# A third seven-product block in the wide products of three feed-forward steps, shared sums written back into their banks, and W_uq's rope columns multiplied once

## The chip, the cores and the metric

One Trainium2 chip, one core of it. The metric is the time of one execution of the whole program on the device in microseconds (us), the lower the better. The core works with several engines side by side: TensorE (PE in the profile; its weight loads are PEld), VectorE (DVE), ScalarE (ACT), GpSimd (POOL), and SyncE (SP), which issues nearly all transfers (DMAs) here. Each engine runs its own instructions in a fixed order and waits for others by semaphores.

## What is computed

A decoder trunk of two layers for 256 tokens, width 1024, in fp32:

```python
h = h + 0.5 * swiglu(rms_norm(h, ffn1_norm), ffn1_w_gate, ffn1_w_up, ffn1_w_down)   # D_FF = 2816
u = rms_norm(h, mix_norm)
...  # proj = u @ w_in; stick-breaking attention (8 heads of 64)
q = (rms_norm(c_q, q_lat_norm) @ w_uq).reshape(b, s, MLA_HEADS, MLA_QK_DIM)     # 4 heads of 128 + 64
q_nope, q_rope = q[..., :MLA_NOPE_DIM], q[..., MLA_NOPE_DIM:]
q_rope = apply_rope(q_rope, cos[:, None, :], sin[:, None, :])
...  # latent attention, output projection
h = h + 0.5 * swiglu(rms_norm(h, ffn2_norm), ffn2_w_gate, ffn2_w_up, ffn2_w_down)
gate = jax.nn.sigmoid(rms_norm(h, ple_norm) @ w_ple_gate)
h = h + gate * (p_i @ w_ple_proj)
```

`swiglu(x)` is `(silu(x @ w_gate) * (x @ w_up)) @ w_down`, and `apply_rope` turns the two halves of 32 of each 64: `x1*cos - x2*sin` and `x2*cos + x1*sin`.

## The kernel before

The work is a sequence of four feed-forward steps (tags a0, b0, a1, b1, here steps 1 to 4), each layer's mixing stage behind its first step and its per-layer embedding behind its second. The 256 tokens are two halves of 128, and a block of outputs is 512 columns wide, the last of the six blocks 256.

**Products.** fp32 is made of three products of a faster format: each operand is split in a high part and the rest, and `mm3` (L255 to L266) issues three matmuls, wh·xh (L262), wl·xh (L263) and wh·xl (L264). A weight tile of 128x1024 takes one DMA of 512 KB into a raw buffer (7 of them), an ACT copy that rounds it to wh (L158, or L199 in a seven-product), and a DVE subtraction wl = raw − wh (L159 or L200). wh and wl have 8 buffers each. PE needs both.

**A plain block** of gate and up: 8 weight tiles, 96 matmuls of 512 columns into four banks of PSUM (g and u for each half of the tokens). Then ACT makes silu(g) (L565), DVE the product pr (L569) and its transpose (L541); a DMA into memory and four back (L543, L548) turn it, and ACT and DVE split the turned tile into fh and fl (L524, L525). DVE also adds up sums of turned tiles for the down projection (L485 to L497).

**A wide seven-product block** (`wide_seven`, L599) replaces a part of these products by the seven products of a 2 x 2 block scheme (Strassen-Winograd): the halves of the tokens and of the inner dimension on one side; a gate and an up tile on the other. Four weight tiles of class `Seven` become seven operands by four sums of raw tiles on DVE (L194), in the order 1, 7, 6, 5, 2, 4, 3 (`operands_own_first`, L220). Products 1, 7, 6 and 5 start the banks p1, p7, p6 and p5; 2 adds onto p1, 4 onto p7, 3 onto p5. Sums that several outputs share are made beside the banks: u is a copy of p1 (ACT, L613), then DVE adds p6 to u (L615), makes v = u + p7 (L616) and e = p5 − v (L618). The other half of the inner dimension comes as ordinary products (`half_mm`, L621): the gate unit ug onto p1 and p7, the up unit uu onto p5 and onto a fresh bank c22. DVE finishes the outputs with v = u + p7 (L628), u = p5 − u (L631) and e = e + c22 (L632). The block has 90 matmuls, and 11 instead of 8 subtractions for wl. `wide_sevens` (L53) names the blocks that are done in this way: 3 in the first step, 1 and 3 in the others. The down projection uses sevens of its own (`SEVEN`), which the change leaves alone.

**W_uq in the mixing stage** (L903 to L921). `qs` are four banks. Its eight groups of 128 columns, each with two `mm3` of 256 columns, are four groups for the nope part, two for the rope part (qs[2]) and two for the same rope columns in rotated order (qs[3]). DVE makes r1 = qs[2]·cos (L917) and r2 = qs[3]·sin (L919), the sign of the rotation in the sine's table, and POOL adds both to qr (L921), which the scores (L945 and after) use beside kn (L930) and qn (L912). Later the attention's output is normed (L882), turned by PE (L893) and projected.

**What sets the order.** The program is written as one sequence; a scheduler places the instructions of each engine by priorities, with hand-set due times (`soon`, `tick`, counted in PE time, L255 ff.) for the pieces that follow a block, such as the turning of pr. `r(1.4)` moves that piece later by 1.4 us.

## Time and profile before

| | |
|---|---|
| three runs | 989.3, 989.6 and 990.46 us, median 989.6 |
| the profiled execution | 989.71 us, of which the span is 987.9 us |
| mean granted clock of PE | 0.997 |
| PE, DVE, ACT busy | 977.5, 850.4, 652.3 us |
| matmuls | 4904 |
| 512 KB weight tiles loaded | 338, 5.2 us from issue to landing |

The span is the time from the first to the last instruction of the profiled execution; 1.8 us lie around it. Rows of the timeline are start, duration, engine, line, operation, output <- inputs and shape; a bracket at the end is idle time ahead of the row and what ended it. An "x2" means two instructions in one row. Names in the trace leave out numbers: all tiles of steps 2 and 4 have a b, those of steps 1 and 3 an a. Durations of neighbours on one engine can overlap, since a pipeline starts the next before the last has ended, so what an instruction costs is read from the starts.

### The profile page before, as it was taken

The page shows a single profiled execution, that of the slowest core. Times are in us where ns is not written, and L with a number is a line of the kernel's source. Part 1 is how long each engine was busy: PE and PEld are TensorE (multiplying, and loading weights), DVE is VectorE, ACT ScalarE, POOL GpSimd, SP SyncE. Part 2 cuts the span into 40 slices and gives each one's busy share as a digit, 9 for nine tenths or more (in the row PEclk, how much of TensorE's full clock was granted, in tenths as well). Part 3 has the DMA queues.
Part 4 walks back from the last instruction along what each step waited for, and adds up shares of the span by engine and source line. Part 5 has one row for each costly group of instructions (what it writes and reads, how often), then busy time and mean ns, then how long its engine had stood idle before and what let it go on. Part 6 is the DMA issues. An engine that isn't in the chain of part 4 may idle for free.

```text
span 987.9 us, 14025 instructions
## 1 busy us (share of the span) xinstructions
PE 977.5 (99%) x4904; PEld 826.0 (84%) x4904; DVE 850.4 (86%) x1130; ACT 652.3 (66%) x1003; POOL 9.3 (1%) x13
## 2 busy tenths in 40 slices
PE   9999999999999999999999999999999999999996
PEld 7888888899888888888888888889998888888885
DVE  5799899966779998999889989998676899989994
ACT  5856566857577566657876655667766766656673
POOL 0000000000100000000000000000010000000000
PEclk9999999999999999999999999999999999999998
DMA  8948766765244788666647776668623367876641
GB/s 292 337 183 290 247 200 218 252 236 169 77 138 140 252 261 302 172 227 233 214 139 281 232 270 210 211 226 291 208 87 128 107 214 249 282 235 205 219 163 43
DMA packets 85175, 208.40 MB, mean 211 GB/s; under 512 B 13680, under 2 KB 33264, under 8 KB 85104
## 3 DMA queue, kind: packets, MB, share of 16 engines
q1 hardware_dynamic: 84672, 206.93, 62.5%
q8 instruction: 38, 0.62, 0.3%
q10 hardware_dynamic: 432, 0.57, 0.2%
q14 instruction: 33, 0.27, 0.1%
HBM read 195.94 MB, written 11.53 MB: 210 GB/s over the span
## 4 chain that ended last, share of the span: by engine, by line
PE 91%; ACT 3%; DVE 3%; DMA 2%; issue 1%; SPq 0%; ACTq 0%; DVEq 0%
PE p_b L262 3%; PE p_b L264 3%; PE p_b L263 3%; PE p_a L262 3%; PE p_a L264 3%; PE p_a L263 3%; PE d_a L264 3%; PE d_b L262 3%; PE d_b L263 3%; PE d_a L263 3%; PE d_a L262 3%; PE d_b L264 3%; PE g_b L262 3%; PE g_b L263 3%; PE g_b L264 3%; PE g_a L264 2%
## 5 line engine op out<-in xcount | busy, mean ns | idle before, releaser
L159 DVE TENSOR_TENSOR wl<-raw,wh 128x1024 fp32r<-128x1024 f32 (+1 forms) x278 | 324.3, 1191 | 61.8 <-ACT wh L158 58.5
L158 ACT ACTIVATE wh<-raw 128x1024 fp32r<-128x1024 f32 (+1 forms) x278 | 281.9, 1038 | 109.0 <-DMA raw<-in_w 21.1
L199 ACT ACTIVATE wh<-raw 128x1024 fp32r<-128x1024 f32 x133 | 139.2, 1059 | 112.7 <-DVE raw L194 70.4
L200 DVE TENSOR_TENSOR wl<-raw,wh 128x1024 fp32r<-128x1024 f32 x133 | 160.8, 1219 | 9.9 <-ACT wh L199 8.1
L194 DVE TENSOR_TENSOR raw<-raw,raw 128x1024 f32<-128x1024 f32 x76 | 92.3, 1219 | 2.0 <-DMA raw<-in_w 1.5
L262 PE MATMUL d_b<-wh,fh_b 128*128 128x512 f32 x108 | 42.4, 392 | 0.0
L262 PE MATMUL d_a<-wh,fh_a 128*128 128x512 f32 x108 | 42.4, 392 | 0.0
L264 PE MATMUL d_b<-wh,fl_b 128*128 128x512 f32 x108 | 42.1, 389 | 0.0
L264 PE MATMUL d_a<-wh,fl_a 128*128 128x512 f32 x108 | 42.1, 389 | 0.0
L263 PE MATMUL d_a<-wl,fh_a 128*128 128x512 f32 x108 | 42.0, 389 | 0.0
L263 PE MATMUL d_b<-wl,fh_b 128*128 128x512 f32 x108 | 42.0, 389 | 0.0
L262 PE MATMUL g_a<-wh,x0h 128*128 128x512 f32 x80 | 31.3, 393 | 0.0
L263 PE MATMUL g_a<-wl,x0h 128*128 128x512 f32 x80 | 31.1, 391 | 0.2 <-DVE wl L159 0.2
L264 PE MATMUL g_a<-wh,x0l 128*128 128x512 f32 x80 | 31.0, 390 | 0.0
L263 PE MATMUL u_a<-wl,x0h 128*128 128x512 f32 x64 | 25.2, 393 | 0.2
L262 PE MATMUL g_b<-wh,x_mix0h 128*128 128x512 f32 x64 | 25.0, 391 | 0.0
L262 PE MATMUL g_b<-wh,x_mix1h 128*128 128x512 f32 x64 | 25.0, 391 | 0.0
L263 PE MATMUL g_b<-wl,x_mix1h 128*128 128x512 f32 x64 | 25.0, 391 | 0.0
L262 PE MATMUL g_a<-wh,xe0h 128*128 128x512 f32 x64 | 25.0, 391 | 0.0
L263 PE MATMUL g_b<-wl,x_mix0h 128*128 128x512 f32 x64 | 25.0, 391 | 0.0
L262 PE MATMUL u_a<-wh,x0h 128*128 128x512 f32 x64 | 24.9, 392 | 0.0
L264 PE MATMUL u_a<-wh,x0l 128*128 128x512 f32 x64 | 24.9, 390 | 0.0
(561 smaller groups left out, 2681.7 us busy)
## 6 DMA issues: line engine op xcount, KB each, us to landing
raw<-in_w SPq DMA_DIRECT2D x338, 512.0 KB, 5.2
m_b<-pr_b SPq DMA_DIRECT2D x20, 256.0 KB, 2.5
ft_b<-m_b SPq DMA_DIRECT2D x80, 64.0 KB, 3.0
raw<-in_w SPq DMA_DIRECT2D x16, 256.0 KB, 4.5
m_a<-pr_a SPq DMA_DIRECT2D x16, 256.0 KB, 2.4
ft_a<-m_a SPq DMA_DIRECT2D x64, 64.0 KB, 2.7
xin<-in_xT SPq DMA_DIRECT2D x4, 256.0 KB, 5.1
h<-in_xr SPq DMA_DIRECT2D x2, 512.0 KB, 8.9
```

Of the source, the lines that this page charges most:

```text
L158: nc.scalar.activation(wh[:, a], r[:, a], AF.Copy),
L159: nc.vector.tensor_tensor(wl[:, a], r[:, a], wh[:, a].bitcast(F32), ALU.subtract),
L194: nc.vector.tensor_tensor(self.raw[o], self.raw[a], self.raw[b], op)
L199: newest_wh[0] = nc.scalar.activation(wh, r, AF.Copy)
L200: nc.vector.tensor_tensor(wl, r, wh.bitcast(F32), ALU.subtract)
L262: nc.tensor.matmul(o, ah, bh, start=start, stop=False, **kw)
L263: nc.tensor.matmul(o, ah, bl, start=False, stop=False, **kw)
L264: newest_mm[0] = nc.tensor.matmul(o, al, bh, start=False, stop=stop, **kw)
```

## The change

Three things change.

1. `wide_sevens` adds block 4 in steps 2 to 4, so the three steps have sevens at 1, 3 and 4. Step 1 keeps block 3.
2. In every wide seven the sums are written back into banks: u = u + p6 and v = u + p7 as before; then ACT copies v into bank p7, DVE writes p5 − v into bank p6 and p5 − u into bank p5. From there on all products (2, 4, 3 and both halves of `half_mm`) add onto the four banks, and silu and pr read the banks themselves. The bank c22, the tile e and the three late DVE sums are gone; the delay of 1.4 us is gone too.
3. W_uq is multiplied without the rotated columns (six groups, not eight; the weight unit is filled up with zeros). r2 is made of four DVE operations of 32 partitions, each of which reads the neighbouring group of 32 rows of qs[2]; the sine's table has its signs swapped.

```diff
-    return (3,) if first else (1, 3)
+    return (3,) if first else (1, 3, 4)
...
-            e2 = tuple(f_p.tile([P, 4, T], F32, tag=f"f5{q}", name=f"c{q}_{tag}{i}").rearrange("p a b -> p (a b)") for q in "hl")
-            u, v, e = e2[0][:, :512], e2[0][:, 512:], e2[1][:, :512]
+            e2 = f_p.tile([P, 4, T], F32, tag="f5h", name=f"c_{tag}{i}").rearrange("p a b -> p (a b)")
+            u, v = e2[:, :512], e2[:, 512:]
...
                 elif q == 6:
                     nc.vector.tensor_tensor(u, u, p[6], ALU.add)
                     nc.vector.tensor_tensor(v, u, p[7], ALU.add)
+                    nc.scalar.copy(p[7], v)
                 elif q == 5:
-                    nc.vector.tensor_tensor(e, p[5], v, ALU.subtract)
-            c22 = bank(f"c22_{tag}{i}")
+                    nc.vector.tensor_tensor(p[6], p[5], v, ALU.subtract)
+                    nc.vector.tensor_tensor(p[5], p[5], u, ALU.subtract)
...
-                        mm3(banks[t], tok(x, 4 + k, t), u.at(k, 0, 512), banks[t] is c22 and k == 0, k == 3, skip_group_check=True)
+                        mm3(banks[t], tok(x, 4 + k, t), u.at(k, 0, 512), False, k == 3, skip_group_check=True)
...
             half_mm(ug, (p[1], p[7]))
-            nc.vector.tensor_tensor(v, u, p[7], ALU.add)
-            rests = [gated(i, 0, p[1], u)[1], gated(i, 1, v, e)[1]]
-            half_mm(uu, (p[5], c22))
-            nc.vector.tensor_tensor(u, p[5], u, ALU.subtract)
-            nc.vector.tensor_tensor(e, e, c22, ALU.add)
+            rests = [gated(i, 0, p[1], p[5])[1], gated(i, 1, p[7], p[6])[1]]
+            half_mm(uu, (p[5], p[6]))
             for r in rests:
-                r(1.4)
+                r()
...
-        qs = [pair(f"uq{L}_{i}") for i in range(4)]
-        for m in range(8):
+        qs = [pair(f"uq{L}_{i}") for i in range(3)]
+        for m in range(6):
...
-        nc.vector.tensor_tensor(r2, qs[3], bc(rc[:, 1], 2), ALU.mult)
+        for a in range(4):
+            to, of = (slice(32 * b, 32 * b + 32) for b in (a, a ^ 1))
+            nc.vector.tensor_tensor(r2[to], qs[2][of], rc[of, 1].unsqueeze(1).to_broadcast([32, 2, T]), ALU.mult)
...
-        units.append(cols(uq, np.r_[nope, rope, rotd]))
+        u = np.zeros((P, 2, UNIT // 2), uq.dtype)
+        u[:, :, :768] = cols(uq, np.r_[nope, rope]).reshape(P, 2, 768)
+        units.append(u.reshape(P, UNIT))
...
-    c[:, C_SIN : C_SIN + T] = np.concatenate([-sin, sin] * 2)
+    c[:, C_SIN : C_SIN + T] = np.concatenate([sin, -sin] * 2)
```

The scheduler answers to this with another order. First DVE in step 2, where block 2 ends and block 3 begins. A name holds the tile, the step (b0 is step 2), the block and the half; `wl7_59_3` is the operand in raw buffer 3 of the seven whose first weight unit is 59 (block 3), `wl61_0_0` the first tile of weight unit 61 (block 3's gate half), and pr_b0_20 the product of block 2, first half. Before:

```order
L200 TENSOR_TENSOR wl7_59_0_149_3598<-raw7_59_0_3523,wh7_59_0_149_3597 128x1024
L493 TENSOR_TENSOR sxl_b0_3398<-sum1_b0_1_3400,sxh_b0_3397 128x512
L200 TENSOR_TENSOR wl7_59_3_150_3622<-raw7_59_3_3538,wh7_59_3_150_3621 128x1024
L569 SCALAR_TENSOR_TENSOR pr_b0_20_3503<-u_b0_20_3329,hr_mix0_2812,s_b0_20_3427 128x512
L569 SCALAR_TENSOR_TENSOR pr_b0_21_3511<-u_b0_21_3330,hr_mix0_2812,s_b0_21_3429 128x512
L541 STREAM_TRANSPOSE pr_b0_20_3503<-pr_b0_20_3503 128x512
L541 STREAM_TRANSPOSE pr_b0_21_3511<-pr_b0_21_3511 128x512
L159 TENSOR_TENSOR wl61_0_0_151_3633<-raw61_0_0_151_3634,wh61_0_0_151_3632 128x1024
```

And DVE at the same place after the change:

```order
L493 TENSOR_TENSOR sxl_b0_3382<-sum1_b0_1_3384,sxh_b0_3381 128x512
L194 TENSOR_TENSOR raw7_59_0_3506<-raw7_59_0_3506,raw7_59_2_3569 128x1024
L569 SCALAR_TENSOR_TENSOR pr_b0_20_3487<-u_b0_20_3313,hr_mix0_2799,s_b0_20_3411 128x512
L569 SCALAR_TENSOR_TENSOR pr_b0_21_3495<-u_b0_21_3314,hr_mix0_2799,s_b0_21_3413 128x512
L541 STREAM_TRANSPOSE pr_b0_20_3487<-pr_b0_20_3487 128x512
L541 STREAM_TRANSPOSE pr_b0_21_3495<-pr_b0_21_3495 128x512
L200 TENSOR_TENSOR wl7_59_0_149_3583<-raw7_59_0_3506,wh7_59_0_149_3582 128x1024
L200 TENSOR_TENSOR wl7_59_3_150_3607<-raw7_59_3_3521,wh7_59_3_150_3606 128x1024
L616 TENSOR_TENSOR c_b03_3505<-c_b03_3505,p6_b03_3503 128x512
L159 TENSOR_TENSOR wl61_0_0_151_3617<-raw61_0_0_151_3618,wh61_0_0_151_3616 128x1024
```

The two last wl of block 3's seven-product stood ahead of the products of block 2 and now stand behind them. Next PE in block 4 of step 2. Before, a plain block begins there with

```order
L262 MATMUL g_b0_40_3725<-wh63_0_0_155_3729,x_mix0h_2809 128x512
L263 MATMUL g_b0_40_3725<-wl63_0_0_155_3730,x_mix0h_2809 128x512
L264 MATMUL g_b0_40_3725<-wh63_0_0_155_3729,x_mix0l_2810 128x512
L262 MATMUL g_b0_41_3726<-wh63_0_0_155_3729,x_mix0h_2809 128x512
L263 MATMUL g_b0_41_3726<-wl63_0_0_155_3730,x_mix0h_2809 128x512
```

After the change, the place where its seven-product gives way to the ordinary half (p1, p7, p6 and p5 are the banks, unit 63 belongs to the seven, 65 and 66 to the gate and up half):

```order
L264 MATMUL p7_b04_3707<-wh7_63_0_160_3787,x_mix0l_2797 128x512
L262 MATMUL p7_b04_3707<-wh65_0_0_162_3827,x_mix0h_2796 128x512
L262 MATMUL p6_b04_3708<-wh66_0_0_164_3867,x_mix0h_2796 128x512
L263 MATMUL p5_b04_3709<-wl7_63_3_161_3818,xsh_b0_3110 128x512
L264 MATMUL p5_b04_3709<-wh7_63_3_161_3817,xsl_b0_3111 128x512
L262 MATMUL p5_b04_3709<-wh7_63_3_161_3817,xsh_b0_3110 128x512
L263 MATMUL p5_b04_3709<-wl7_63_3_161_3818,xsh_b0_3110 128x512
L264 MATMUL p5_b04_3709<-wh7_63_3_161_3817,xsl_b0_3111 128x512
L262 MATMUL p5_b04_3709<-wh66_0_0_164_3867,x_mix0h_2796 128x512
L263 MATMUL p1_b04_3706<-wl65_0_0_162_3828,x_mix0h_2796 128x512
```

Matmuls with wh stand ahead of those with the wl of the same tile, several operands apart. The matmul with wl65_0_0_162 (the last row here) is the 137th from block 3's first. The third place is DVE in the first layer's mixing stage, before:

```order
L882 TENSOR_SCALAR on1_sb0_2464<-ov0_1_2312,tss_sb0_2450 128x512
L917 TENSOR_TENSOR r10_2536<-uq0_2_2468,rc0_2533 128x512
L919 TENSOR_TENSOR r20_2538<-uq0_3_2469,rc0_2533 128x512
L930 TENSOR_TENSOR kn0_2542<-kn0_0_2543,rl0_2423 128x512
L930 TENSOR_TENSOR kn0_2542<-kn0_1_2557,rl0_2423 128x512
```

and after:

```order
L881 TENSOR_SCALAR on1_sb0_2461<-ov0_1_2309,tss_sb0_2447 128x512
L916 TENSOR_TENSOR r10_2520<-uq0_2_2465,rc0_2517 128x512
L921 TENSOR_TENSOR r20_2522<-uq0_2_2465,rc0_2517 32x512 x4
L932 TENSOR_TENSOR kn0_2529<-kn0_0_2530,rl0_2420 128x512
L932 TENSOR_TENSOR kn0_2529<-kn0_1_2544,rl0_2420 128x512
```

One row on qs[3] has become four on groups of 32 rows of qs[2], ahead of both kn.

More of the change, by code (lines that the diff above doesn't have):

```diff
@@ L1184, in _weights @@
         rope = np.concatenate([192 * h + 128 + ar(64) for h in range(4)])
-        rotd = np.concatenate([192 * h + 128 + rot for h in range(4)])
-        units.append(cols(uq, np.r_[nope, rope, rotd]))
+        u = np.zeros((P, 2, UNIT // 2), uq.dtype)
+        u[:, :, :768] = cols(uq, np.r_[nope, rope]).reshape(P, 2, 768)
+        units.append(u.reshape(P, UNIT))
         ukv = i["w_ukv"][L]
```

## The prediction

> **What bounds the kernel now.** I read the page first: busy times, the clock row, the chain that ended last.
>
> ```profile
> PE 977.5 (99%) x4904; PEld 826.0 (84%) x4904; DVE 850.4 (86%) x1130; ACT 652.3 (66%) x1003; POOL 9.3 (1%) x13
> PEclk9999999999999999999999999999999999999998
> PE 91%; ACT 3%; DVE 3%; DMA 2%; issue 1%; SPq 0%; ACTq 0%; DVEq 0%
> ```
>
> TensorE (PE) is busy 99% of the 987.9 us span, at full clock, and carries 91% of the chain. Any matmul that goes should shorten the run by its pitch. But VectorE (DVE) is busy 86%, and 86% is a mean. So next I asked for busy time by windows of 10 us around block 3 of step 2 (columns: PE, weight loads, DVE, ACT, POOL busy, each with its count; clock; DMA share; GB/s).
>
> ```profile
> 340.00:350.00 10.00, 10.00 (x46) 8.29 (x45) 9.93 (x13) 6.51 (x9) 0.00 (x0) 1.00 0.73 235
> 350.00:360.00 10.00, 10.00 (x46) 8.29 (x45) 10.00 (x15) 7.31 (x9) 0.00 (x0) 1.00 0.78 256
> 360.00:370.00 10.00, 10.00 (x46) 8.29 (x45) 10.00 (x14) 6.02 (x8) 0.00 (x0) 1.00 0.79 239
> 370.00:380.00 10.00, 10.00 (x46) 8.29 (x45) 10.00 (x16) 6.90 (x9) 0.00 (x0) 1.00 0.84 322
> 380.00:390.00 10.00, 10.00 (x45) 8.27 (x45) 6.44 (x7) 5.65 (x7) 0.00 (x0) 1.00 0.88 258
> ```
>
> This is the reading that decides. Around one seven-product block DVE has no idle time for 40 us; it catches up only in the plain block behind it, after 380. Block 4, which is to become a seven-product block too, is that plain block.
>
> **Pitches.** The timeline of both engines there (start, duration, engine, line, instruction):
>
> ```profile
> 339.69 0.39 PE L263 MATMUL g_b<-wl,x_mix0h 128*128 128x512 f32 x1
> 354.20 0.39 PE L264 MATMUL u_b<-wh,x_mix0l 128*128 128x512 f32 x1
> 355.11 0.39 PE L262 MATMUL p_b<-wh,x_mix0h 128*128 128x512 f32 x1
> 375.51 0.39 PE L262 MATMUL g_b<-wh,x_mix0h 128*128 128x512 f32 x1
> 355.20 1.40 DVE L569 SCALAR_TENSOR_TENSOR pr_b<-u_b,hr_mix,s_b 128x512 f32<-128x512 f32 x2
> 356.52 1.29 DVE L541 STREAM_TRANSPOSE pr_b<-pr_b 128x512 f32<-128x512 f32 x2
> 357.74 2.31 DVE L159 TENSOR_TENSOR wl<-raw,wh 128x1024 fp32r<-128x1024 f32 x2
> 359.97 0.68 DVE L615 TENSOR_TENSOR ch_b<-ch_b,p_b 128x512 f32<-128x512 f32 x1
> 360.57 1.22 DVE L159 TENSOR_TENSOR wl<-raw,wh 128x1024 fp32r<-128x1024 f32 x1
> 361.71 0.68 DVE L616 TENSOR_TENSOR ch_b<-ch_b,p_b 128x512 f32<-128x512 f32 x1
> 344.90 1.22 DVE L194 TENSOR_TENSOR raw<-raw,raw 128x1024 f32<-128x1024 f32 x1
> 346.04 0.68 DVE L525 TENSOR_TENSOR fl_b<-ft_b,fh_b 128x512 fp32r<-128x512 f32 x1
> 346.64 1.22 DVE L194 TENSOR_TENSOR raw<-raw,raw 128x1024 f32<-128x1024 f32 x1
> 369.52 0.42 DVE L485 TENSOR_TENSOR sum_b<-ft_b 128x256 f32<-128x256 f32 x1
> 369.86 0.42 DVE L487 TENSOR_TENSOR sum_b<-ft_b,ft_b 128x256 f32<-128x256 f32 x1
> 378.86 2.32 DVE L159 TENSOR_TENSOR wl<-raw,wh 128x1024 fp32r<-128x1024 f32 x2
> ```
>
> Durations overlap, so I take start-to-start pitches. PE: 68 matmuls of 512 columns lie between 339.69 and 355.11, which is 0.2268 us each; the 90 of block 3 take 375.51 − 355.11 = 20.40, the same. DVE: a wl or a sum of two raw tiles 1.14 (360.57 to 361.71; 344.90 to 346.04), a 512-wide operation 0.60 (359.97 to 360.57), a 256-wide one 0.34 (369.52 to 369.86), pr 1.32 and the transpose 1.22 for the two (355.20 to 356.52, 356.52 to 357.74). A check: the order of before has, from the first pr to the wl at 378.86, 4 pr, 4 transposes, 10 wl, 9 512-wide and 5 256-wide operations: 2.64 + 2.44 + 11.40 + 5.40 + 1.70 = 23.58; the trace has 378.86 − 355.20 = 23.66. The sum of pitches is good to under 1%.
>
> **PE: three blocks.** A plain block has 96 matmuls, a seven-product one 90. Block 4 in three steps: 3 × 6 × 0.2268 = −4.08 us. Nothing else of the write-back touches PE's work, as the two halves that went to a bank of their own now add onto p5 and p6.
>
> **PE: W_uq.** 24 matmuls of 256 columns go, 12 a layer:
>
> ```profile
> 247.40 0.28 PE L263 MATMUL uq<-xqf5h,wh 128*128 128x256 f32 x1
> 253.03 0.28 PE L262 MATMUL kn<-xqf4l,wh 128*128 128x256 f32 x1
> 252.47 0.68 DVE L917 TENSOR_TENSOR r<-uq,rc 128x512 f32<-128x512 f32 x1
> 253.30 0.69 DVE L919 TENSOR_TENSOR r<-uq,rc 128x512 f32<-128x512 f32 x1
> 253.96 1.41 DVE L930 TENSOR_TENSOR kn<-kn,rl 128x512 f32<-128x512 f32 x2
> 256.74 0.39 PE L945 MATMUL s<-kn,qn 128*128 128x128 f32 x2
> 274.82 0.88 DVE L882 TENSOR_SCALAR on_mla<-os,tss_mla 128x512 f32<-128x512 f32 x2
> 275.79 0.60 PE L893 MATMUL yt_mla<-c_sb,on_mla 128*128 128x128 f32 x4
> ```
>
> 47 matmuls in 5.63 us, 0.1198 each, so PE reaches s 12 × 0.1198 = 1.44 earlier, at 255.3. But on DVE one r becomes four of 32 partitions; a row costs by its columns, so I take 0.60 each, and 0.69 as the upper bound. The first can follow the r at 252.47 at 253.07, the fourth ends its pitch at 255.47, and the two kn then end by 256.9 instead of 255.37. The first is done near 256.2, so PE waits some 0.9 and keeps 0.5. Even that has to pass a tie: on_mla ends at 275.70 and PE uses it at 275.79, at the end of a chain of softmax and norm, into which the new order puts two more wl. I take 0 per layer, with bounds of −1.44 (all of it counts) and +1.0 (the chain moves by the delay of kn). [...]
>
> **The write-back itself.** In blocks 1 and 3, v is now final after p6 and goes to bank p7 by an ACT copy. Product 4 adds onto p7 and so waits for this. Two rows show where before waited at that place:
>
> ```profile
> 320.04 0.50 PE L262 MATMUL p_b<-wh,x_mix0h 128*128 128x512 f32 x1
> 805.81 0.50 PE L262 MATMUL p_b<-wh,x_mix1h 128*128 128x512 f32 x1
> ```
>
> Those are late by 0.2 to 0.3 us, behind DVE in steps 2 and 4. In the new order product 4 stands six matmuls further back (1.36 us later), and by the pitches p7 is written at 8.65 us after the block's first matmul, against 38 × 0.2268 = 8.62 for its use: I take −0.25 for each of the two, bounds −0.3 and +0.5. DVE has two bank operations fewer per block. −0.5 together.
>
> **DVE in steps 2 and 4.** In the order after, from the first pr of block 2 up to wl65_0_0_162, the first weights of block 4 that belong to no seven-product, DVE has 4 pr, 4 transposes, 14 wl, 4 sums of raw tiles, 8 bank operations, 4 other 512-wide and 13 256-wide operations: 2.64 + 2.44 + 15.96 + 4.56 + 4.80 + 2.40 + 4.42 = 37.2 us. The first pr waits for the last matmul of u_b_20, three before the end of block 2 (354.20 + 0.39 = 354.59 in the timeline of before, 0.5 ahead of block 3's first matmul at 355.11). In front of that pr DVE has run dry: two wl of block 3 that stood ahead of it now stand behind, so DVE can't use the time up to u_b's end. wl65_0_0_162 is thus there 37.2 − 0.5 = 36.7 us after block 3's first matmul. PE, in its new order, asks for it 136 matmuls after that one: 136 × 0.2268 = 30.8. The difference, 5.9 us, is a stall of PE. The same sum gives 3.2 at wl7_63_0_160, so it comes in several pieces, none above 3 us. Behind wl65_0_0_162 each wl (1.14) feeds 12 matmuls (2.72), and DVE is ahead again. Two such steps: +12 us.
>
> What could hide it is a lead of DVE at that point. A lead would need free weight buffers: there are 8, and PE sets them free. ACT shows this in before, where its copy waits for PE's matmul:
>
> ```profile
> 336.32 1.06 ACT L199 ACTIVATE wh<-raw 128x1024 fp32r<-128x1024 f32 x1 [1.66 <-PE g_b L264]
> ```
>
> **DVE in step 3.** There the order keeps both wl of block 3 ahead of the first pr and puts the last sums of the down projection behind wl7_101_3_255. Up to that one DVE has 4 pr, 4 transposes, 11 wl, 4 sums, 8 bank operations, 3 512-wide and 5 256-wide ones, 30.5 us, so it is ready at 30.0; PE asks for it after 130 matmuls, at 29.5. I take +0.6, bounds 0 and +3.
>
> **Sum**, against the profiled execution's 989.7 us (the runs' median is 989.6, so the two agree): 989.7 − 4.1 − 0.5 + 0 + 12 + 0.6 = 997.7; I say 997.5 us. What a measurement can tell here from no change is about 0.2%, 2 us.
>
> **Rivals.**
> - *PE stays the only bound.* DVE keeps some 6 us more lead than the order lets me see, and all 42 matmuls count: 989.7 − 4.1 − 2.9 = 982.7, faster. For it: PE is 99% busy, and DVE has 3.6 us of 10 to spare after 380. Against: the pr that waits for u_b stands in front of the work that would build the lead. It decides if DVE gets through the 37.2 us in 31. Chance 0.17.
> - *Half the stall.* Part of the wl go faster or earlier, 3 us a step remain: 989.7 − 4.6 + 6 = 991.1, up to 994. Chance 0.13.
> - *A worse stall.* On SP's queue the raw tile of W 63_3 stands behind the transfers that turn block 2's products, and ACT copies into p7 in order, ahead of copies of weights that PE needs. What a late tile costs, the table of waits shows (total us, times, longest):
>
> ```profile
> ACT wh L158 <- DMA raw<-in_w: 21.1, 16, 4.3
> ```
>
>   The mean is 1.3 us. Two such waits in each of steps 2 to 4 give 997.7 + 3 × 2.6 = 1005.5 us; the longest in each gives 1010. Against: by the order the tile is asked for some 9 us (by the pitches) before DVE's turn to use it. The granted clock is 1.00 in every window above, so before shows no price of PE's gaps beyond their own length. [...] Chance 0.13.
> - *The change doesn't do what it says*: excluded by the order, which has 42 matmul rows fewer on PE.
>
> **How the numbers follow.** The forecast has 0.57, and by its own bounds (W_uq ± 2, write-back +1, step 3 +2.4, stall ± 2) 993 to 1003. The range reaches over half the stall (990) and to the worse stall (1006); what it leaves out is the first rival and the far end of the third. Faster by over 0.2%: the first rival and the edge of the second, 0.18. Within 0.2% (987.7 to 991.7): part of the second, 0.07. Slower: 0.75.
>
> **What would show it.** In the trace after, PE should have gaps of 1 to 3 us within block 4 of steps 2 and 4 (near 376 to 400 and 860 to 885), released by DVE wl (L200, then L159), about 6 us in each step; DVE should be busy 10.00 in every window of the 35 us before; step 3 should show at most 1 us; block 1's 0.3 us should be gone. In the mix, PE should wait for kn ahead of s by about 1 us. I am wrong if those gaps sum to less than 4 us in each step, or if DVE is not at 10.00 there; then PE's 7 us come through.

## The result, and the profile after

| | before | after |
|---|---|---|
| median of four runs | 989.65 us | 1012.86 us (1012.01 to 1013.83) |
| ratio to before, 95% interval | | 1.0234 (1.022 to 1.0247) |
| span of the profiled execution | 987.9 us | 1010.7 us |
| mean granted clock of PE | 0.997 | 0.993 |

The change costs 23.2 us. The forecast was 997.5 us, slower by 8, and its range ended at 1006: the sign was right and the size was off by a factor of three. The busy times, the clock row and the chain, from the page of after:

```profile
PE 983.6 (97%) x4862; PEld 822.0 (81%) x4862; DVE 875.8 (87%) x1155; ACT 663.3 (66%) x1025; POOL 8.5 (1%) x13
PEclk9999999999999999999999999999999999989999
PE 80%; DVE 11%; DMA 3%; issue 3%; ACT 3%; SPq 0%; DVEq 0%; ACTq 0%; POOL 0%; POOLq 0%
```

PE has the 42 matmuls fewer and is busy for longer, DVE's share of the chain has gone from 3% to 11%, and one slice of the clock row, in step 4, has dropped. The waits that PE itself shows are small. Total us, times and the longest, from the table of waits of after:

```profile
PE p_b L263 <- DVE wl L159: 4.3, 2, 2.2
PE s L947 <- DVE kn L932: 2.7, 2, 1.4
PE p_b L262 <- ACT wh L199: 2.6, 4, 0.8
PE yt_mla L892 <- DVE on_mla L881: 1.5, 2, 0.8
```

These come to 11.1 us. A wait before one matmul leaves out that the matmul behind it can take longer (0.50 us instead of 0.39 at 382.17 in step 2) and whatever a lower clock takes. So I compared the two executions by stages: from the first matmul of a stage to that of the next. Each entry is the stage's time less that in before, in us, from the profiled executions (the kernels beside after are told below; "b3-5" are blocks 3 to 5 of a step, "down" its down projection):

| stage (before, us) | after | no block 4 | old W_uq | W_uq alone | write-back alone | no block 4 in step 3 | block 4 without its sums | block 4 alone |
|---|---|---|---|---|---|---|---|---|
| mix 1 (109.30) | +1.74 | +1.74 | +0.03 | +1.75 | +0.03 | +1.77 | +1.76 | 0 |
| step 2, b0-2 (62.14) | −0.18 | −0.18 | −0.21 | −0.14 | −0.15 | −0.20 | −0.18 | −0.01 |
| step 2, b3-5 (53.04) | +5.33 | +0.29 | +5.90 | +0.20 | +1.81 | +5.54 | +0.85 | +1.90 |
| step 2, down (56.67) | +0.01 | +0.01 | +1.11 | +0.01 | +0.01 | +0.01 | +0.43 | +2.29 |
| embedding, layer 1 (33.86) | +0.41 | −0.21 | +0.79 | +0.06 | +0.46 | +0.07 | +2.11 | +0.23 |
| step 3, b3-5 (53.13) | −0.01 | +0.08 | −0.03 | −0.05 | +0.08 | +0.08 | −1.07 | +1.93 |
| step 3, down (56.69) | +6.32 | 0 | +6.12 | 0 | 0 | 0 | −0.03 | +1.18 |
| mix 3 (109.52) | +1.97 | +1.79 | +0.47 | +2.08 | +0.07 | +1.80 | +2.04 | +0.21 |
| step 4, b0-2 (62.16) | −0.20 | −0.20 | −0.22 | −0.17 | −0.23 | −0.20 | −0.20 | −0.03 |
| step 4, b3-5 (53.04) | +7.28 | 0 | +4.13 | +0.20 | +0.10 | +7.30 | +0.54 | +3.49 |
| step 4, down (56.69) | −0.01 | −0.01 | +0.17 | 0 | −0.01 | −0.01 | +0.17 | +0.59 |
| embedding, layer 2, to the end (37.30) | +0.49 | +0.10 | +0.42 | −0.02 | +0.13 | +1.12 | +2.37 | +1.37 |
| whole run, median (us) | 1012.86 | 994.49 | 1008.41 | 992.65 | 991.03 | 1007.44 | 996.51 | 1003.53 |

Three stages of after hold 18.93 of the 22.8 us by which the spans differ, and the two mixing stages 3.71. Step 2's entry is near the one that was forecast (5.9 − 1.36 = 4.5); step 3's stands in its down projection, where the forecast did not look.

**Step 2.** Windows of 10 us in after, as before (PE, weight loads, DVE, ACT, POOL, clock, DMA share, GB/s):

```profile
340.00:350.00 10.00, 10.00 (x46) 8.28 (x45) 6.59 (x7) 4.10 (x6) 0.00 (x0) 1.00 0.75 214
350.00:360.00 10.00, 10.00 (x46) 8.29 (x45) 10.00 (x17) 6.67 (x9) 0.00 (x0) 1.00 0.55 205
...
380.00:390.00 10.00, 7.82 (x29) 4.76 (x28) 9.96 (x12) 8.10 (x10) 0.00 (x0) 1.00 0.65 214
390.00:400.00 10.00, 7.84 (x35) 6.17 (x35) 10.00 (x16) 7.65 (x11) 0.00 (x0) 1.00 0.77 256
```

DVE is full from 350 on and PE loses 4.3 us of busy time between 380 and 400, in the place that was forecast. But between 340 and 350 DVE has 3.4 us idle. The timeline of DVE in after, at that idle time and at the two ends of the queue that the prediction summed:

```profile
343.43 2.48 DVE L194 TENSOR_TENSOR raw<-raw,raw 128x1024 f32<-128x1024 f32 x2 [3.34 <-DMA raw<-in_w]
356.30 1.41 DVE L569 SCALAR_TENSOR_TENSOR pr_b<-u_b,hr_mix,s_b 128x512 f32<-128x512 f32 x2
392.43 1.21 DVE L159 TENSOR_TENSOR wl<-raw,wh 128x1024 fp32r<-128x1024 f32 x1
```

From the first pr to the end of the last wl's pitch is 392.43 + 1.14 − 356.30 = 37.27 us; the sum of pitches gave 37.2. The idle time in front is a wait for a weight tile. SP's queue in after shows why: the turn of block 1 (m_b) is issued, and only behind it the tile.

```profile
327.85 1.48 SPq L191 DMA_DIRECT2D raw<-in_w  x2
336.14 1.07 SPq L543 DMA_DIRECT2D m_b<-pr_b  x2
337.31 0.40 SPq L191 DMA_DIRECT2D raw<-in_w  x1
```

Before issued three tiles ahead of that turn, which left at 336.21 there too:

```profile
325.79 4.89 SPq L191 DMA_DIRECT2D raw<-in_w  x3
```

**Step 4.** The same pieces, and a lower clock. Windows of after, and then PE's timeline:

```profile
880.00:890.00 10.00, 8.28 (x26) 5.47 (x25) 9.32 (x12) 8.09 (x10) 0.00 (x0) 0.83 0.63 212
890.00:900.00 10.00, 7.84 (x27) 5.94 (x28) 10.00 (x16) 6.39 (x10) 0.00 (x0) 0.83 0.71 222
```

```profile
881.39 0.50 PE L262 MATMUL p_b<-wh,xsh_b 128*128 128x512 f32 x1 [0.81 <-ACT wh L199]
882.34 0.49 PE L262 MATMUL p_b<-wh,x_mix1h 128*128 128x512 f32 x1 [0.45 <-ACT wh L199]
883.29 0.58 PE L263 MATMUL p_b<-wl,xsh_b 128*128 128x512 f32 x1 [0.46 <-DVE wl L200]
883.66 0.63 PE L264 MATMUL p_b<-wh,xsl_b 128*128 128x512 f32 x1
884.09 0.63 PE L262 MATMUL p_b<-wh,xsh_b 128*128 128x512 f32 x1
...
893.65 0.67 PE L263 MATMUL p_b<-wl,x_mix1h 128*128 128x512 f32 x1 [2.16 <-DVE wl L159]
```

The pitch is 884.09 − 883.66 = 0.43 instead of 0.2268 us, and the granted clock is 0.50 there (883.58 to 887.00, the last section). So a window of 10 us whose mean clock is 0.83 has had half clock for 3.4 us (10 × 0.17 × 2).

**Step 3.** In before, SP issued the first four tiles of the down projection's first seven-product at 590.12, 22.4 us ahead of the projection's first matmul at 612.53:

```profile
590.12 1.85 SPq L191 DMA_DIRECT2D raw<-in_w  x4
```

In after the projection begins at 619.5, and the tiles go out at 604.63 and 606.45 (one row), 611.63 and 621.83. SP waited 4.5 us in two waits ahead of the first two, for DVE's wl, which set the raw buffers free; the third stands behind the turn of block 4 (610.61), and the last behind that of block 5:

```profile
604.63 2.14 SPq L191 DMA_DIRECT2D raw<-in_w  x2
...
611.63 0.40 SPq L191 DMA_DIRECT2D raw<-in_w  x1
...
620.55 1.18 SPq L543 DMA_DIRECT2D m_a<-pr_a  x2
621.83 0.38 SPq L191 DMA_DIRECT2D raw<-in_w  x1
```

DVE waits for it, then ACT, then PE, whose clock falls to half here too (0.50 from 637.82 to 641.23, so 0.89 in the window from 630). The timeline of DVE in after, and the window in which it waits:

```profile
626.17 2.49 DVE L194 TENSOR_TENSOR raw<-raw,raw 128x1024 f32<-128x1024 f32 x2 [2.70 <-DMA raw<-in_w]
```

```profile
620.00:630.00 10.00, 9.52 (x43) 7.58 (x42) 6.39 (x10) 4.95 (x7) 0.00 (x0) 1.00 0.59 165
```

DVE is busy for 6.39 of these 10 us. So in this place PE does not wait for work that DVE is still at, as in block 4 of step 2: DVE itself has nothing to work on, since the tile is late.

### The profile page after: what moved, and what is told of

Its sections match the earlier page's. It is cut to its first block, busy times and chain, and to the rows that moved or that the text cites. A ratio compares the mean times of both kernels' runs of the same rounds, so it can differ in the third digit from the quotient of the medians.

```text
span 1010.7 us, 13970 instructions
## 1 busy us (share of the span) xinstructions
PE 983.6 (97%) x4862; PEld 822.0 (81%) x4862; DVE 875.8 (87%) x1155; ACT 663.3 (66%) x1025; POOL 8.5 (1%) x13
## 4 chain that ended last, share of the span: by engine, by line
PE 80%; DVE 11%; DMA 3%; issue 3%; ACT 3%; SPq 0%; DVEq 0%; ACTq 0%; POOL 0%; POOLq 0%
PE p_a L263 4%; PE p_a L264 4%; PE p_a L262 3%; PE p_b L263 3%; PE p_b L264 3%; PE g_a L262 3%; PE p_b L262 3%; PE g_a L264 3%; PE g_a L263 3%; DMA raw<-in_w 3%; PE d_a L263 2%; PE d_a L264 2%; PE d_a L262 2%; PE d_b L264 2%; PE d_b L263 2%
## 5 line engine op out<-in xcount | busy, mean ns | idle before, releaser
L199 ACT ACTIVATE wh<-raw 128x1024 fp32r<-128x1024 f32 x154 | 159.9, 1056 | 133.6 <-DVE raw L194 100.2
L200 DVE TENSOR_TENSOR wl<-raw,wh 128x1024 fp32r<-128x1024 f32 x154 | 185.1, 1218 | 13.3 <-ACT wh L199 12.4
L194 DVE TENSOR_TENSOR raw<-raw,raw 128x1024 f32<-128x1024 f32 x88 | 107.2, 1219 | 11.8 <-DMA raw<-in_w 11.1
L263 PE MATMUL p_b<-wl,x_mix1h 128*128 128x512 f32 x66 | 26.9, 407 | 2.2 <-DVE wl L159 2.2
L263 PE MATMUL p_b<-wl,x_mix0h 128*128 128x512 f32 x66 | 26.0, 394 | 2.6 <-DVE wl L159 2.2
L262 PE MATMUL p_b<-wh,x_mix1h 128*128 128x512 f32 x66 | 26.5, 406 | 0.4 <-ACT wh L199 0.4
L262 PE MATMUL p_b<-wh,x_mix0h 128*128 128x512 f32 x66 | 26.0, 396 | 0.5 <-ACT wh L199 0.4
L264 PE MATMUL p_b<-wh,x_mix1l 128*128 128x512 f32 x66 | 26.5, 404 | 0.0
L263 PE MATMUL p_a<-wl,xe0h 128*128 128x512 f32 x66 | 25.9, 393 | 0.4 <-DVE wl L200 0.4
L264 PE MATMUL p_a<-wh,xe0l 128*128 128x512 f32 x66 | 25.7, 389 | 0.0
L262 PEld LDWEIGHTS d_a<-wh,fh_a 128*128 128x128 f32 x108 | 20.4, 190 | 6.4 <-ACT wh L199 1.6
```

The lines of the kernel that those rows point to most:

```text
L194: nc.vector.tensor_tensor(self.raw[o], self.raw[a], self.raw[b], op)
L199: newest_wh[0] = nc.scalar.activation(wh, r, AF.Copy)
L200: nc.vector.tensor_tensor(wl, r, wh.bitcast(F32), ALU.subtract)
L262: nc.tensor.matmul(o, ah, bh, start=start, stop=False, **kw)
L263: nc.tensor.matmul(o, ah, bl, start=False, stop=False, **kw)
L264: newest_mm[0] = nc.tensor.matmul(o, al, bh, start=False, stop=stop, **kw)
```

## The experiments

Each median stands beside before in runs on the same chip (989.5 to 989.6 us). The diffs are against the kernel named ahead of them.

### Which part costs what

**After without block 4 as a seven-product.**

```diff
-    return (3,) if first else (1, 3, 4)
+    return (3,) if first else (1, 3)
```

> The changed kernel with the sevens at blocks 1 and 3 again: write-back and W_uq's edit alone. Theory A (the loss has separate places: about 5 us in blocks 3 and 4 of step 2, 6 in the down projection of step 3, 7 in blocks 3 and 4 of step 4, all from block 4; and 1.7 to 2.0 in each mixing stage, from W_uq's edit): the mixing stages keep their loss, the rest goes, 992 to 993.5 us. Rival B (block 4 takes weight buffers and moves the whole order, the mixing stages with it): all of the loss goes and W_uq's 24 matmuls begin to count, 986 to 988 us. The forecast on record (mixing stages at 0, write-back -0.5): 989.2 us.

Measured: 994.49 us, ratio 1.0048 (1.0033 to 1.0063). Block 4 makes 1012.86 − 994.49 = 18.4 of the 23.2 us; the rows b3-5 and down of steps 2 to 4 lose nothing without it (at most 0.3). But 994.49 − 989.51 = 5.0 us stay, which the forecast had at −0.5; the next runs divide them.

**After with the W_uq of before**, and **before with the W_uq edit alone.** The second edit:

```diff
-        qs = [pair(f"uq{L}_{i}") for i in range(4)]
-        for m in range(8):
+        qs = [pair(f"uq{L}_{i}") for i in range(3)]
+        for m in range(6):
...
-        nc.vector.tensor_tensor(r2, qs[3], bc(rc[:, 1], 2), ALU.mult)
+        for a in range(4):
+            to, of = (slice(32 * b, 32 * b + 32) for b in (a, a ^ 1))
+            nc.vector.tensor_tensor(r2[to], qs[2][of], rc[of, 1].unsqueeze(1).to_broadcast([32, 2, T]), ALU.mult)
```

> The changed kernel with W_uq as before (eight groups, one r2): block 4 and write-back. Theory A: only the mixing stages' loss goes, 1012.9 - 3.7 = 1009.2 us. Rival B: the mixing stages' loss stays, as it came from the order that block 4 sets, and 24 matmuls come back: 1013 to 1016 us. The forecast on record: 997.7 us, W_uq at 0.

> The kernel before with W_uq's edit alone. Theory A: 1.7 to 2.0 us lost in each mixing stage, 993.4 us. The forecast on record: 0 per layer, 989.7. Rival (PE is the only bound, 24 matmuls of 0.12 count): 986.8 us.

Measured: 1008.41 us, ratio 1.0187 (1.017 to 1.0204), and 992.65 us, ratio 1.0033 (1.002 to 1.0046). W_uq's edit costs 3.1 us alone and 4.5 within the change, though it takes 24 matmuls away. All of it alone stands in the two mixing stages (+1.75, +2.08). The timeline of after in the first of them shows two places. The first is the rope products:

```profile
252.80 2.79 DVE L921 TENSOR_TENSOR r<-uq,rc 32x512 f32<-32x512 f32 x4
255.62 1.29 DVE L932 TENSOR_TENSOR kn<-kn,rl 128x512 f32<-128x512 f32 x2
256.46 0.46 PE L947 MATMUL s<-kn,qn 128*128 128x128 f32 x2 [1.37 <-DVE kn L932]
```

Four operations take 2.82 us start to start, 0.70 each and not the 0.60 of a 512-wide operation on 128 partitions; each lasts 0.68 to 0.70, so nothing overlaps. PE's 1.37 us for kn eat nearly all of the 1.44 that the 12 matmuls gave. The second place is the end of the attention, some 20 us later:

```profile
274.40 1.06 ACT L158 ACTIVATE wh<-raw 128x1024 fp32r<-128x1024 f32 x1
275.49 1.23 DVE L159 TENSOR_TENSOR wl<-raw,wh 128x1024 fp32r<-128x1024 f32 x1 [1.24 <-ACT wh L158]
277.21 0.88 DVE L881 TENSOR_SCALAR on_mla<-os,tss_mla 128x512 f32<-128x512 f32 x2
277.85 1.18 PE L892 MATMUL yt_mla<-c_sb,on_mla 128*128 128x128 f32 x8 [0.77 <-DVE on_mla L881]
```

Copies and subtractions of the next weights, 1.06 and 1.23 us each, now stand among the small steps of the softmax and the norm, ACT's and DVE's. on_mla starts at 277.21 (274.82 in before), and PE waits for it.

**Before with W_uq's edit and these weights moved behind that chain**, to tell whether it is their place. Two of the four weight units of the projection are made ready only behind a fence after the norm:

```diff
-        for u in us[:3]:
+        for u in us[:2]:
             u.ready()
...
         fence[:] = newest
+        for u in us[2:]:
+            u.ready()
```

> The kernel before with W_uq's edit alone, and the last four weight tiles of the output projection made after the norm of the latent attention, so that no wh and no wl stands inside softmax and norm. Theory A (the 1.75 us in each mixing stage of W_uq alone come from three wh and two wl that its new order puts among the exponentials and inside the norm): they go, while the wait for kn (1.4) eats what 12 matmuls save: 989 to 990 us. Rival B (the wait for kn and the four r2 are the loss): 992 to 993 us, as for W_uq alone.

Measured: 992.02 us, ratio 1.0023 (1.0013 to 1.0033). The mixing stages are where they were in before (−0.06, −0.08), so the place of those weights was the cause there (the wait for kn, 1.37 us, is still paid, against the 1.44 saved). The total hardly follows: step 2's blocks 3 to 5 lose 0.46, its down projection 0.81, the embedding stages 1.20 and 0.50. It is a miss as a remedy. That the work moved back is what comes late in those stages was not followed up.

**Before with the write-back alone** (W_uq of before, sevens at 1 and 3; the diff is the one of the front part, without its first and last pieces).

> The kernel before with the write-back alone (sevens at 1 and 3, W_uq as before). Theory A and the forecast on record: 0.2 us less in block 1 of steps 2 and 4, 989.0 to 989.3 us. Rival (the ACT copy into p7 and its wait cost): 0.3 to 0.5 us in each of the seven blocks, 991 to 993 us.

Measured: 991.03 us, ratio 1.0018 (1.0008 to 1.0027), 1.5 us slower. The 0.2 in block 1 of steps 2 and 4 came as forecast (−0.15, −0.23); step 2's blocks 3 to 5 lose 1.81. DVE's timeline of this kernel shows the late tile of after once more:

```profile
342.51 2.49 DVE L194 TENSOR_TENSOR raw<-raw,raw 128x1024 f32<-128x1024 f32 x2 [3.24 <-DMA raw<-in_w]
```

**The same with DVE writing p7 in place of ACT.**

```diff
-                    nc.scalar.copy(p[7], v)
+                    nc.vector.tensor_tensor(p[7], u, p[7], ALU.add)
```

> The kernel before with the write-back alone, as measured at 991.0 us, but VectorE writes u + p7 into bank p7 a second time where ACT copied v. Theory A (the 1.5 us of the write-back alone are waits for the ACT copy, which stands in ACT's order behind copies of weights): 989 to 990 us. Rival B (they come from elsewhere, such as the order of VectorE's queue ahead of block 3): 991 us or more.

Measured: 991.49 us, ratio 1.0017 (1.0007 to 1.0026). The copy on ACT is not the cause. The same edit in after:

> The changed kernel with the same edit: VectorE writes bank p7, not ACT. Theory A (VectorE's queue): 0.6 us more in each of the two sevens, 1.2 us more stall in each of steps 2 and 4; but in step 3 the last tile of the down projection's first seven is issued ahead of the turns of block 5, so 4 to 6 us of its 6.3 go: 1008 to 1011 us. Rival B (ACT's in-order copy into p7 is what PE waits for): 1005 us or less, with the gain in steps 2 and 4.

Measured: 1011.12 us, ratio 1.0214 (1.0185 to 1.0242): the interval overlaps that of after. The stages changed (step 2 b3-5 +7.83, step 3 b3-5 +2.73 and down +3.07), the total did not.

**The write-back alone, with the weight tile ahead of the turn.** The turn of block 1 is held on SP until the third raw tile of block 3's seven-product has been issued:

```diff
-            nc.sync.dma_start(m, pr.rearrange("p (q r) -> p q r", q=4))
+            turns[self.tag, i, t] = nc.sync.dma_start(m, pr.rearrange("p (q r) -> p q r", q=4))
...
             for q, (wh, wl) in Seven().operands_own_first():
+                if q == 7 and i == 3 and (tag, 1, 0) in turns:
+                    after(turns[tag, 1, 0], newest_load[0])
```

> The write-back alone (991.0 us; 1.8 us of it in blocks 3 and 4 of step 2 in its trace), with one order more: the transfer that starts the turn of block 1's first product waits on SP until the third tile of block 3's seven is issued, as it stood in the kernel before. Theory A (the write-back costs nothing by itself; it lets block 1's turn overtake that tile on SP, VectorE waits 3.2 us for the tile, and two of block 3's wl slide behind block 2's products): 989.0 to 989.6 us, with VectorE's wait ahead of block 3 gone. Rival B (p7 by way of VectorE and ACT is the cost): 991 us.

Measured: 990.08 us, ratio 1.0006 (0.9997 to 1.0015): no difference from before, and step 2's b3-5 at +0.17. The timeline of SP and of DVE in this kernel:

```profile
326.86 4.00 SPq L191 DMA_DIRECT2D raw<-in_w  x3
```

```profile
339.00 2.48 DVE L194 TENSOR_TENSOR raw<-raw,raw 128x1024 f32<-128x1024 f32 x2
```

The sums start at 339.00, without a wait. The write-back's cost was the order of two issues on SP: in the schedule the turn of block 1's product stands ahead of a weight tile, and the tile comes late. The turn itself leaves at the same time as in before (336.14 and 336.21); what moved it in the schedule, such as the dropped delay of 1.4 us, no run separates.

### Block 4: order or amount of work

**After without block 4 in step 3 alone.**

```diff
-    return (3,) if first else (1, 3, 4)
+    return (3,) if first else (1, 3) if third else (1, 3, 4)
```

> The changed kernel, but step 3 keeps its sevens at blocks 1 and 3. In the trace of the changed kernel blocks 3 and 4 of step 3 take as long as before, and its down projection 6.3 us longer. Theory A (block 4 keeps raw buffers longer, so the down projection's first tiles are queued on SP behind the turns of blocks 4 and 5): the 6.3 us go, 1006.5 us. Rival B (the down projection's loss comes from the write-back or from a clock that falls at random, not from block 4 of this step): 1011 to 1014 us.

Measured: 1007.44 us, ratio 1.0181 (1.0166 to 1.0197). Step 3's down projection is at 0 again, the other stages stay. So the +6.32 there are block 4's, paid one stage later.

**Before with block 4 alone**, without write-back and with the old W_uq (the first piece of the change's diff).

> The kernel before with the third seven alone: blocks 1, 3 and 4, sums beside the banks as before, W_uq as before. Theory A (the third seven is the loss, by VectorE's queue; the order keeps two wl of block 3 ahead of the first pr, and step 3's loads ahead of the turns): stalls of 4 to 6 us in steps 2 and 4 against 4.1 us of matmuls saved in all, 994 to 999 us. Rival B (the write-back is what makes a third seven cheaper, since without it each seven has two more bank operations and a fifth bank): slower than the 1008.4 us of block 4 with write-back.

Measured: 1003.53 us, ratio 1.0144 (1.0127 to 1.0161), 13.9 us slower, between its two forecasts. The third seven-product costs in the form of before too, spread over other stages (step 2: 1.90 + 2.29, step 3: 1.93 + 1.18, step 4: 3.49 + 0.59).

**After with the raw sums of block 4 left out.** Its four operands are split unsummed, so this kernel leaves the scheme's sums out and its products are not the block's; DVE saves 4 × 1.14 = 4.56 us in each of three blocks, and loads, buffers, copies and matmuls stay:

```diff
-            nc.vector.tensor_tensor(self.raw[o], self.raw[a], self.raw[b], op)
+            if self.sums:
+                nc.vector.tensor_tensor(self.raw[o], self.raw[a], self.raw[b], op)
...
-            for q, (wh, wl) in Seven().operands_own_first():
+            for q, (wh, wl) in Seven(i < 4).operands_own_first():
```

> The changed kernel without the four sums of raw tiles in block 4 of steps 2 to 4 (that block's operands are left unsummed; all matmuls, loads and wl stay). Theory A (VectorE's queue between block 2 and block 4 is the bound in steps 2 and 4): 4 x 1.14 = 4.6 us leave that queue, the stall of 6.5 falls to about 2 in each, the half clock of step 4 goes, and the order of loads in step 3 is that of before, so its 6.3 go too: 995 to 997 us. Rival B (tiles that come late by DMA, or ACT's in-order copies, set the stall): steps 2 and 4 keep 5 to 7 us each, 1004 us or more.

Measured: 996.51 us, ratio 1.0064 (1.0046 to 1.0082), 16.4 us less than after for 13.7 us less of DVE's work. Blocks 3 to 5 and down together are at +1.28, −1.10 and +0.71 instead of +5.34, +6.31 and +7.27. A window of this kernel at block 4 of step 2:

```profile
385.00:395.00 10.00, 8.36 (x37) 6.62 (x36) 7.91 (x13) 3.67 (x7) 0.00 (x0) 1.00 0.86 282
```

DVE has idle time again at 385, and the clock stays at 1.00. What is left of PE's loss is another wait, for a bank. ACT's copy into p7 stands there behind a wh that waits 2.52 us for its tile:

```profile
388.16 0.50 PE L264 MATMUL p_b<-wh,x_mix0h 128*128 128x512 f32 x1 [1.64 <-ACT p_b L620]
```

In step 2 this decides for DVE's queue: DVE still waits 3.23 us for the late tile at 343.63, as in after, and yet the stall of block 4 goes when DVE has less to do. (A sum also ties an operand to a second tile; that wait goes with it.) Two limits belong to the total. In step 3 the four tiles of the projection go out at 597.06 here, so the work and the order changed together. And the two embedding stages lose 4.48 instead of 0.90 together, where PE waits for DVE (2.8 us in two waits): of the 18.0 us that the rows of steps 2 to 4 gain, 3.6 come back there.

**Two ways to take work off.** GpSimd makes wl of the two gate and up halves (4 tiles in each seven-product of steps 2 to 4):

```diff
-                    nc.vector.tensor_tensor(wl[:, a], r[:, a], wh[:, a].bitcast(F32), ALU.subtract),
+                    self.by.tensor_tensor(wl[:, a], r[:, a], wh[:, a].bitcast(F32), ALU.subtract),
...
-            ug, uu = Unit(4), Unit(4)
+            ug, uu = (Unit(4, by=nc.gpsimd if feed is None else None) for _ in range(2))
```

> The changed kernel; GpSimd instead of VectorE makes the wl of the four ordinary tiles of each seven in steps 2 to 4. Theory A (VectorE's queue between block 2 and block 4 is the bound in steps 2 and 4): four or five wl of 1.14 leave that queue, 4.6 us off each stall of 6.5, the half clock of step 4 (about 1.9) goes with it, and the order of loads in step 3 is that of before: 995 to 1000 us. Rival B (two engines that read the same memory hinder each other, or GpSimd at some 2.6 us per tile, twice its 1.30 for 512, is late for PE): the stalls stay or move to GpSimd, 1008 us or more.

Measured: 1022.24 us, ratio 1.0339 (1.0321 to 1.0357), worse than after by 9.4. The timeline of GpSimd and of DVE in this kernel:

```profile
359.07 11.44 POOL L160 TENSOR_TENSOR wl<-raw,wh 128x1024 fp32r<-128x1024 f32 x4 [31.91 <-DVE pr_b L570]
```

```profile
362.50 0.68 DVE L617 TENSOR_TENSOR c_b<-c_b,p_b 128x512 f32<-128x512 f32 x1
365.21 3.06 DVE L201 TENSOR_TENSOR wl<-raw,wh 128x1024 fp32r<-128x1024 f32 x1
368.19 4.66 DVE L195 TENSOR_TENSOR raw<-raw,raw 128x1024 f32<-128x1024 f32 x2
```

One wl costs GpSimd 2.86 us, and in that time DVE's own wl takes 3.06 and a raw sum 2.33, where 1.22 is usual. An operation with an operand in PSUM keeps its 0.68. What GpSimd takes over, DVE loses again. PE's longest waits in this run are for ACT's copy into p7 (10.2 us in three), whose operand DVE makes late: in block 4 of step 2 behind a wl that took 2.77.

And the turns issued by GpSimd, so that SP's weight tiles stand behind none of them:

```diff
-            nc.sync.dma_start(m, pr.rearrange("p (q r) -> p q r", q=4))
+            nc.gpsimd.dma_start(m, pr.rearrange("p (q r) -> p q r", q=4))
...
-                    nc.sync.dma_start(a[32 * q : 32 * q + 32], m[:, q].rearrange("(a f) r -> f a r", a=4))
+                    nc.gpsimd.dma_start(a[32 * q : 32 * q + 32], m[:, q].rearrange("(a f) r -> f a r", a=4))
```

> The changed kernel; the transfers that turn the products are issued by GpSimd instead of SP, so no weight tile stands behind them. Theory A (loads behind turns on SP cost 6.3 us in step 3's down projection, and 3.3 us of VectorE's time ahead of block 3 in step 2, where it waited for a tile): step 3's loss goes, and up to 3.3 in each of steps 2 and 4: 1000 to 1006.5 us. Rival B (the tiles are late since the buffers come free late, or because the transfers themselves are full): within 2 us of 1012.9.

Measured: 1047.99 us, ratio 1.0581 (1.0552 to 1.0611). Issued there, each half of the turn lands later. KB each and us to landing, from the page of this kernel (the four transfers back, ft_b, take 3.9 us as well):

```profile
m_b<-pr_b POOLq DMA_DIRECT2D x20, 256.0 KB, 3.9
```

Both are 2.2 in after.

This run tells nothing on the order of the loads, since it made the turns slower.

**After with the loads ahead of the turns.** By now my theory was that the late tiles set block 4's cost: what had cured the write-back should cure a good part of after. First the hold of block 1's turn in every wide step (the diff shown above, in after):

> The changed kernel with the same order: in steps 2 to 4 the tile of block 3's seven goes ahead of block 1's turn on SP. Theory A (of the stall of 6.5 us in step 2, 2.3 are the two wl behind the first pr, which follow from the late tile, and the rest is the mere amount of VectorE's work): stalls of about 4 us in steps 2 and 4, 4 to 7 us less in all with the half clock of step 4; step 3's down projection keeps its 6.3: 1006 to 1009 us. Rival B (the late tile is the whole cause): the stalls go, 1000 us or less. Rival C (the order ahead of block 3 does not matter): 1012 us or more.

Measured: 1013.21 us, ratio 1.0235 (1.0221 to 1.0249), the same as after. Yet step 2's and step 4's blocks 3 to 5 lose nothing any more (+0.11, +0.08): block 3's sums come in time, DVE has its lead, and of block 4's stall 1.4 to 1.5 us are left, as much as its matmuls save. In their down projections +5.98 and +4.38 are lost instead. SP and DVE of this kernel, in step 2:

```profile
410.21 1.19 SPq L544 DMA_DIRECT2D m_b<-pr_b  x2
411.49 0.38 SPq L191 DMA_DIRECT2D raw<-in_w  x1
```

```profile
415.98 2.48 DVE L194 TENSOR_TENSOR raw<-raw,raw 128x1024 f32<-128x1024 f32 x2 [2.84 <-DMA raw<-in_w]
```

It is step 3's picture of after: a tile of the down projection stands behind a turn, DVE waits 2.84 us for it, and the projection starves. As in step 3, DVE is not full there: in the 10 us from 406 it is busy for 4.67.

**The same, and in step 3 the turn of block 4 held until four tiles of the projection's first seven-product are issued**; then **this with the W_uq of before.**

```diff
             self.load(b12)
+            if hold in turns:
+                after(turns[hold], newest_load[0])
             self.sum(b12, b12, b22)
```

> The changed kernel with that order and a second one: in step 3 the turn of block 4 waits on SP until the four tiles of the down projection's first seven are issued. Theory A (the 6.3 us of step 3's down projection are these tiles behind the turns of blocks 4 and 5): 6.3 us less than with the first order alone, 1000 to 1003 us. Rival B (the tiles are late since their buffers come free late): no change against the first order alone.

> The same two orders with W_uq as before: what is left is the third seven alone, with its write-back and without the order faults. Theory A: 3.5 us less than with the edit of W_uq, 996 to 999 us, still 6 to 9 us slower than before, as VectorE's work in blocks 3 and 4 exceeds PE's. Rival B (without the order faults the 18 matmuls saved count): 985 to 989 us.

Measured: 1012.46 us, ratio 1.0225 (1.0211 to 1.0239), and 1003.51 us, ratio 1.014 (1.0126 to 1.0154), above both of its forecasts. In the first, step 3's projection still loses 5.45: its first seven-product is in time now, and the tiles of its second one come late. SP and ACT of this kernel:

```profile
625.92 6.56 SPq L552 DMA_DIRECT2D ft_a<-m_a  x8
632.53 1.85 SPq L193 DMA_DIRECT2D raw<-in_w  x4
```

```profile
637.40 1.06 ACT L201 ACTIVATE wh<-raw 128x1024 fp32r<-128x1024 f32 x1 [3.06 <-DMA raw<-in_w]
```

So holding a turn or two does not cure after: the rivals by which the total stays held, and the stages show that its place moved, to the next tile that stands behind a turn. That the order counts for nothing is not shown. With the W_uq of before the same two holds took 4.9 us off (1008.41 to 1003.51), and no run had every load ahead of the turns. Blocks 3 to 5 and down together, step by step (2, 3, 4), from the profiled executions:

| | step 2 | step 3 | step 4 |
|---|---|---|---|
| after | 5.34 | 6.31 | 7.27 |
| turn of block 1 held | 6.09 | 6.29 | 4.46 |
| both turns held | 5.36 | 5.44 | 3.98 |
| old W_uq | 7.01 | 6.09 | 4.30 |
| both held, old W_uq | 6.04 | 5.18 | 2.85 |
| block 4 alone | 4.19 | 3.11 | 4.08 |
| block 4 without its sums | 1.28 | −1.10 | 0.71 |

The profiled executions of the first two rows with held turns were the quickest of their kernels, 2.2 and 3.2 us below the medians, so their rows show the place better than the size. None of these kernels is faster than before.

What stays open: why block 4 in the form of before, with three late bank operations on DVE in each block, costs less (13.9 us) than in the form of after (1012.86 − 994.49 = 18.4); how much of the loss in the down projections comes from the raw buffers, which come free at DVE's pace, and how much from the turns ahead of the tiles (runs with more buffers weren't tried); and why W_uq of before is worth 4.5 us in after, but 9.0 with both turns held.

## Why the prediction was wrong, step by step

- **PE, −4.1 us for block 4, and −2.9 for W_uq in the first rival.** 42 matmuls are gone, and in after their time shows nowhere as a gain: in every stage concerned something else ended later. Without the raw sums, step 3's blocks 3 to 5 are 1.07 us shorter, of the 1.36 that six matmuls make.
- **DVE's queue in steps 2 and 4: right in step 2.** 37.27 us against 37.2; the stall is 5.33 plus the 1.36 that the block saved, 6.7 against 5.9. PE's pieces came in the place named, none above 2.2: 0.45, 0.44 and 2.15 us for DVE's wl, and 0.84 and 0.45 for ACT's wh, which the prediction did not name. Two of its own signs of being wrong appeared all the same: DVE was at 6.59 in the window from 340, and PE's gaps in step 4 sum to 3.9 us, just under 4 (4.3 in step 2). PE's 7 us did not come through for that. A gap cost more than its length: across the one of 0.84 us the starts are 1.23 apart (380.94 to 382.17), 1.00 above the pitch of 0.2268, and across the one of 0.45 behind it 0.95 (to 383.12), 0.72 above. One reason given was wrong: "In front of that pr DVE has run dry". DVE is at 10.00 in the window ahead of that pr; it had waited 3.34 us already 13 us earlier, for the raw tile that SP issued behind block 1's turn. The two wl that stand behind pr belong to the sums of that late tile; with the tile issued ahead of the turn (the run of 1013.21 us) both stand ahead of pr again, and the stall leaves block 4 and appears in the down projection.
- **Step 4: the clock.** The pieces are those of step 2, with two stretches of half clock, and +7.28 stands beside +5.33. The prediction saw clock 1.00 in its windows of before, and its sum has nothing for the clock. Here no gap was above 2.2, and the clock fell all the same (the last section). After has three stretches of half clock ahead of its last 10 us, two in step 4 and one in step 3's projection, each 3.41 us long at 0.50; they cost at most half of 3.41 each, 5.1 us in all.
- **Step 3, "+0.6, bounds 0 and +3": the step that failed.** Within blocks 3 to 5 it was right: −0.01 is a stall of 1.35 against 1.36 saved. But the sum stopped at wl7_101_3_255, as if what DVE is late with ended where block 4's weights are ready. The loads of the next stage wait for buffers that DVE sets free: the first four tiles of the down projection, which has seven-products of its own, went out from 14.9 us ahead of its first matmul to 2.3 us behind it, where before had the first 22.4 us ahead. The last stood behind block 5's turn, DVE was idle for it, and the projection gave +6.32. The wait that failed the sum is thus one for a transfer, not DVE's own work. The +6.32 is 6 of the 15 us that were missing, and the run without block 4 in step 3 shows that it is block 4's.
- **W_uq, "0 per layer, with bounds of −1.44 and +1.0".** It was +1.74 and +1.97, outside the bounds. The wait for kn was near (1.37 against 0.9; the operations took 0.70, about the bound of 0.69, not the 0.60 taken). The tie at on_mla, which the prediction named, was sized by the delay of kn alone; the weights that the new order puts into that chain cost more than that (without them the mixing stages are at −0.06 and −0.08).
- **Write-back, "−0.5 together".** The −0.2 in block 1 of steps 2 and 4 came. That the new schedule lets a turn overtake a weight tile on SP was not looked for: 1.5 us slower instead.
- **The rival of the worse stall** named SP's queue, but the tile of block 4's seven-product. The tiles that came late were block 3's and the down projection's. Its 1005.5 to 1010 us would have been the nearest.

Summed by the stages of the two profiled executions: 5.33 + 6.32 + 7.28 for block 4 and what hangs on it, 3.71 for the mixing stages and 0.2 for the rest are 22.8 us, where the forecast had +8.

## What to carry to other kernels

When one engine is full for longer than its buffers cover, sum its work up to each operand that the next engine asks for: over 37 us that was good to 0.1 us here. Then go one stage further and follow the loads, which wait for the buffers that the full engine sets free; the stage behind can starve although the engine is idle there. Holding one transfer back mostly moved this loss to the next tile, and less work on the full engine took most of it away. And where an edit moves a transfer forward in the schedule, look at what it now overtakes in the one queue that both share.

## What the runs showed of the hardware

- **Half clock after short gaps.** In step 4 of after the granted clock halved after gaps of 0.81, 0.45 and 0.46 us within 3 us, and again after one of 2.16. Step 2 had the same gaps (0.84, 0.45, 0.45, 2.15) at clock 1.00 throughout, so the gaps alone do not decide it. Nor does PE's idle time in 10 us: in step 2's windows from 380 and 390 it was 2.18 and 2.16 us at clock 1.00, in step 4's from 880 and 890 it was 1.72 and 2.16 at a mean of 0.83. Ahead of the last 10 us of after the clock fell to 0.50 at 637.82, 883.58 and 893.82, each time for 3.41 us. The window of the second fall:

```profile
883.58:887.00 3.42, 3.42 (x9) 2.68 (x9) 2.78 (x5) 3.42 (x5) 0.00 (x0) 0.50 0.69 230
```

  What decides whether the clock falls was not shown.
- **GpSimd and VectorE.** With GpSimd's subtraction running (359.07 to 370.51 and 383.66 to 395.98 in the run of 1022.24 us), DVE's 1024-wide operations on two operands in SBUF took 1.38 to 3.06 us instead of 1.22, and its 512-wide ones with an operand in PSUM 0.68 to 0.70, where before has 0.68.
- **The queue that issues.** The same transfers (m_b and ft_b, medians) landed in 3.9 us when GpSimd issued them, in the run of 1047.99 us, and in 2.2 us when SP did, in after.
